# A float32 transpose of 8192 x 8192: one wait per chunk on TensorE, no branch hint, and another order of two-piece stores

## The chip, the cores and the metric

The kernel runs on one core of one Trainium2 chip. The metric is the device time of one execution in microseconds, from the first to the last work on the core; the smaller the better. Of three runs of the kernel before the median was 1263.56 us, with 1263.29 and 1263.79 at the ends.

## The reference

The input is one float32 matrix of 8192 rows and 8192 columns, 256 MiB, in HBM. The output is its transpose, of the same size. Nothing else is computed:

```python
def setup_inputs():
    return {
        "x": np.random.randn(8192, 8192).astype(np.float32),
    }

def reference(x: np.ndarray) -> np.ndarray:
    return np.transpose(x)
```

So 268 MB have to be read and 268 MB written, with a change of order between.

## The kernel before, in words

**Chunks.** The matrix is cut into two halves of 4096 columns (`s` = 0 and 1), and each half into 64 bands of 128 rows (`c`). A band of a half is a chunk: 128 rows of 16 KB each, 2 MB. There are 128 chunks, first the 64 of `s` = 0, then those of `s` = 1. The place where the second half begins, between chunk 63 and chunk 64, is the seam.

**Loads.** A chunk is loaded by one DMA into one of three input buffers `in0` to `in2`. The first three loads are issued on SyncE's queue, all later ones on ScalarE's (L102). The load of chunk t + 3 is issued once TensorE has finished chunk t and so no longer reads that buffer. The semaphore `s_ld[k]` of a buffer rises by 16 when a load has landed, one for each of the 16 DMA engines that share the transfer.

**TensorE.** It transposes a chunk in 32 pieces of 128 x 128, each a matmul with the identity (L118), into PSUM. The 32 pieces form eight blocks `q` of four. Blocks 0 to 3 go into the half of PSUM that ScalarE empties (`ps0`), blocks 4 to 7 into the half that VectorE empties (`ps1`). Ahead of a chunk stands the wait for its load (L112). Ahead of block 0 and of block 4 stands a wait for the bank (L116): the semaphores `s_banka` and `s_bankv` say that the copy engine has emptied its half of the chunk before. After every second block TensorE raises `s_pe`, on which the copies wait. TensorE's program is a loop, `turns`, of three chunks a turn and 43 turns. At the head of a turn stands a test, `now < 3`, and behind it a branch prefetch hint (L141) for the branch at the loop's end (L147). So the hint is executed in the first three turns.

**Copies.** ScalarE copies blocks 0 to 3 from PSUM into SBUF, VectorE blocks 4 to 7 (L228), each in one to four instructions as the places lie. The place is a region of `regs`, of which there are nine. A region collects one block over eight chunks, so that a row of the output gets 8 x 128 columns, 4 KB, in one piece. The eight blocks are staggered, so that one region becomes full in each chunk. The copy that is a chunk's last on its engine frees the bank.

**Stores.** When a region is full, ScalarE issues its store (L28): 512 rows of the output, 4 KB of each, 2 MB. So in the middle of the kernel ScalarE's queue carries one store and one load per chunk, in turn. In the first chunks the regions hold fewer chunks, and the stores have rows of 512 B, 1 KB and so on.

**The seam.** Seven regions are open when the first half ends. Such a region holds the last columns of 512 output rows and the first columns of 512 other rows. Its store is two DMAs: for block q the first piece has 7 − q chunks and the second q + 1, so rows of (7 − q) x 512 B and (q + 1) x 512 B. In `store` the piece of the first half is issued first. Both raise the region's semaphore, and the region is free when both have landed.

**What sets the order.** Each engine's program is written out by hand in the order shown; there is no scheduler. The transfers on ScalarE's queue start in the order of their issue. The lines that matter are `transposes` (L111 to L124), the loop (L131 to L150), `store` (L160 to L179) and the freeing of the bank (L233 to L238).

Of the kernel before, what the change touches and what calls it, by code (L numbers as in the profile page):

```python
# [40 lines left out]
def kernel(  # L41
# [13 lines left out]
    nc = tc.nc  # L55
# [9 lines left out]
    NIN = 3  # L65
# [4 lines left out]
    with tc.tile_critical():  # L70
        nc.alloc_sbuf_tensor("pad", [P, 32], dt)
        ident = nc.alloc_sbuf_tensor("ident", [P, P], dt).ap()
        ins = [nc.alloc_sbuf_tensor(f"in{k}", [P, J], dt).ap() for k in range(NIN)]
        SIZE = B * W * P
        regs = nc.alloc_sbuf_tensor("regs", [P, NREG * SIZE], dt).ap()
        NH = NR // 2
        pss = [nc.alloc_psum_tensor(f"ps{k}", [P, NH * B * P], dt).ap() for k in range(2)]

        s_id = nc.alloc_semaphore("s_id")
        s_ld = [nc.alloc_semaphore(f"s_ld{k}") for k in range(NIN)]  # L80
        s_st = [nc.alloc_semaphore(f"s_st{k}") for k in range(NREG)]
        s_bank = [nc.alloc_semaphore("s_banka"), nc.alloc_semaphore("s_bankv")]
        s_pe = nc.alloc_semaphore("s_pe")
        s_cp = [nc.alloc_semaphore("s_cpa"), nc.alloc_semaphore("s_cpv")]

        nc.gpsimd.memset(ident, 0.0).then_inc(s_id, 1)  # L86
        nc.gpsimd.wait_ge(s_id, 1)
        nc.gpsimd.affine_select(  # L88
            out=ident,
            in_=ident,  # L90
            compare_op=mybir.AluOpType.not_equal,
            fill=1.0,
            base=0,
            pattern=[[-1, P]],
            channel_multiplier=1,
        ).then_inc(s_id, 1)

        chunks = [(s, c) for s in range(M // J) for c in range(CH)]

        def load(t):  # L100
            s, c = chunks[t]
            (nc.sync if t < NIN else nc.scalar).dma_start(  # L102
                out=ins[t % NIN], in_=x[c * P:(c + 1) * P, s * J:(s + 1) * J]
            ).then_inc(s_ld[t % NIN], 16)

        def transposes(k):  # L111
            nc.tensor.sem_inc(s_ld[k], -16).wait_op(s_ld[k], 16, "sem-ge")  # L112
            for q in range(NR):
                e, g = divmod(q, NH)
                if g == 0:
                    nc.tensor.sem_inc(s_bank[e], -1).wait_op(s_bank[e], 1, "sem-ge")  # L116
                for b in range(B):
                    tr = nc.tensor.transpose(  # L118
                        pss[e][:, (g * B + b) * P:(g * B + b + 1) * P],
                        ins[k][:, q * B * P + b:(q + 1) * B * P - B + b + 1:B],  # L120
                        ident,
                    )
                if q % 2:
                    tr.then_inc(s_pe, 1)  # L124

        T = len(chunks)
        assert T % NIN == NIN - 1
        pe = [nc.tensor.engine]  # L130
        for e in range(2):  # L131
            nc.tensor.sem_inc(s_bank[e], 1)
        nc.tensor.wait_ge(s_id, 2)

        turn = nc.alloc_registers("turn", engines=pe)
        nc.regs_mov(turn, 0)
        nc.br("turns", engines=pe)
        with nc.body("turns", valid_engines=pe):
            now = nc.snap(turn, min_val=0, max_val=T // NIN)
            with nc.tensor.If(now < 3):  # L140
                hint = nc.tensor.mark_branch_hint_location()  # L141
            with nc.tensor.If(now > 0):
                transposes(NIN - 1)
            for k in range(NIN - 1):
                transposes(k)
            nc.regs_alu(turn, turn, 1, op=mybir.AluOpType.add)
            nc.tensor.br_lt(  # L147
                turn, T // NIN + 1, on_true="turns", on_false="done"
            ).branch_hint(hint)
        nc.switch_bb("done")  # L150

        for t in range(NIN):
            load(t)

        copied = [0, 0]
        free = list(range(NREG))
        stored = [0] * NREG
        window = {}

        def store(q, e, count):  # L160
            t0, r, parts = window.pop(q)
            nc.scalar.wait_ge(s_cp[e], count)
            base = 0
            for s, a, z in parts:
                rows = (z - a) * P
                j0 = s * J + q * B * P
                dst = out[j0:j0 + B * P, a * P:a * P + rows]
                dst = dst.rearrange("(q b) i -> q b i", q=P)
                src = regs[:, r * SIZE + base:r * SIZE + base + B * rows]
                base += B * rows  # L170
                if any(stored):
                    st = wide_dma(nc, nc.scalar, "qActDynamicHW", dst, src)
                else:
                    st = nc.scalar.dma_start(
                        out=dst, in_=src.rearrange("q (b i) -> q b i", b=B)
                    )
                st.then_inc(s_st[r], 16)
                stored[r] += 1
            free.append(r)  # L179

        def closes(w, t):
            t0, r, parts = w
            return t + 1 == t0 + sum(z - a for _, a, z in parts)

        for t, (s, c) in enumerate(chunks):
            for e in range(2):
                eng = (nc.scalar, nc.vector)[e]

                place = []
                for q in range(e * NH, (e + 1) * NH):  # L190
                    if q not in window:

                        span = (q - c) % W + 1
                        r = free.pop(0)
                        parts = [(s, c, min(c + span, CH))]
                        if c + span > CH and t + span < T:
                            parts.append((s + 1, 0, c + span - CH))
                        window[q] = (t, r, parts)  # L200
                        if stored[r]:
                            eng.wait_ge(s_st[r], 16 * stored[r])
                    t0, r, parts = window[q]
                    k = [p[0] for p in parts].index(s)
                    base = r * SIZE + B * P * sum(z - a for _, a, z in parts[:k])
                    _, a, z = parts[k]
                    place.append((base + (c - a) * P, (z - a) * P))

                runs = []
                for g in range(NH):  # L210
                    if runs:
                        u = runs[-1]
                        gap = place[g][0] - place[g - 1][0]
                        if place[g][1] == place[u[0]][1] and abs(gap) < 2 ** 15 and (
                            len(u) == 1 or gap == place[u[1]][0] - place[u[0]][0]
                        ):
                            u.append(g)
                            continue
                    runs.append([g])
                for u in runs:  # L220
                    off, dist = place[u[0]]
                    gap = place[u[-1]][0] - place[u[-2]][0] if len(u) > 1 else 0
                    dims = [list(regs.ap[0]), [gap, len(u)], [dist, B], [1, P]]
                    o = bass.AP(regs.tensor, regs.offset + off, dims)
                    i = pss[e][:, u[0] * B * P:(u[-1] + 1) * B * P]
                    i = i.rearrange("p (l b i) -> p l b i", b=B, i=P)
                    eng.wait_ge(s_pe, t * NH + (e * NH + u[-1]) // 2 + 1)  # L227
                    cp = nc.scalar.copy(out=o, in_=i) if e == 0 else nc.vector.tensor_copy(out=o, in_=i)  # L228
                    ends = [e * NH + g for g in u if closes(window[e * NH + g], t)]
                    if ends:  # L230
                        cp.then_inc(s_cp[e], 1)
                        copied[e] += 1
                    if u is runs[-1]:  # L233
                        if ends:
                            eng.wait_ge(s_cp[e], copied[e])
                            eng.sem_inc(s_bank[e], 1)
                        else:
                            cp.then_inc(s_bank[e], 1)  # L238
                    for q in ends:
                        store(q, e, copied[e])  # L240
            if t + NIN < T:
                nc.scalar.wait_ge(s_pe, (t + 1) * NR // 2)
                load(t + NIN)
        for r in range(NREG):
            nc.sync.wait_ge(s_st[r], 16 * stored[r])
# [30 lines left out]
```

## Time and profile before

| what | us |
|---|---|
| median of the runs | 1263.56 |
| lowest and highest | 1263.29, 1263.79 |
| span of the profiled execution | 1261.2 |
| what lies around the span, by the median | 2.4 |
| TensorE busy with matmuls, 4096 of them | 740.3 |
| VectorE busy, 250 copies | 302.7 |
| ScalarE busy, 256 copies | 251.3 |
| DMA: 537 MB in the span | 426 GB/s |

For the profiled execution the span is known; its own time with what lies around it is not listed apart from the three runs, so the 2.4 us are the median less the span.

How to read it: the span runs from the first to the last instruction. A row of the timeline or of the groups gives the line of the kernel, the engine, the operation, what is written and read, and how often. ACTq and SPq are the queues on which ScalarE and SyncE issue DMAs; PEq is TensorE's sequencer. An arrow names what ended an engine's idle time. A row of windows gives the stretch, the busy time of each engine, the granted clock of TensorE, the share of time for which the 16 DMA engines were busy, and the GB/s that they moved.

### The profile page before, as it was taken

What the parts mean: (1) busy time and instruction counts of PE and PEld (TensorE: products, weight loads), DVE (VectorE), ACT (ScalarE), POOL (GpSimd) and SP (SyncE); (2) the same over time, 40 slices, a digit from 0 to 9 for tenths busy, and PEclk for the clock granted to TensorE, in tenths of its full rate; (3) what the DMA queues carried; (4) which work ended last, traced back from release to release, by engine and by line L of the source; (5) the groups of instructions that cost most, each with busy time, mean ns of one, the idle gap of its engine ahead of it and who ended that gap; (6) DMA issues with size and microseconds to landing.
All of it is one profiled execution on the core that took longest, in us unless ns stands there. A gap on an engine that the chain in (4) does not pass through costs nothing. (4 is left out here: it accounts for less than half of the span.)

```text
span 1261.2 us, 9840 instructions
## 1 busy us (share of the span) xinstructions
PE 740.3 (59%) x4096; PEld 719.8 (57%) x4096; DVE 302.7 (24%) x250; ACT 252.6 (20%) x257; POOL 0.7 (0%) x6
## 2 busy tenths in 40 slices
PE   6555655665556565665555655656566655656561
PEld 6555555665556555655555655656566655656561
DVE  3322222222222222222222222222222222222220
ACT  3212121121111211122211121121111211122120
POOL 0000000000000000000000000000000000000000
PEclk9987867777776868687776777676867677777866
DMA  9999999999999999999999999999999999999998
GB/s 386 429 427 426 430 427 429 431 428 430 431 428 431 429 429 430 430 429 430 425 423 419 431 430 429 430 430 429 431 430 429 431 429 430 430 430 429 429 429 351
DMA packets 39273, 536.97 MB, mean 426 GB/s; under 512 B 4320, under 2 KB 4832, under 8 KB 6240
## 3 DMA queue, kind: packets, MB, share of 16 engines
q10 hardware_dynamic: 38832, 530.60, 98.9%
q1 hardware_dynamic: 432, 6.29, 1.2%
q14 instruction: 8, 0.07, 0.0%
q8 instruction: 1, 0.02, 0.0%
HBM read 268.44 MB, written 268.44 MB: 426 GB/s over the span
## 5 line engine op out<-in xcount | busy, mean ns | idle before, releaser
L118 PE MATMUL ps<-ident,in 128*128 128x128 f32 x4096 | 740.3, 363 | 492.9 <-PEq L116 492.9
L118 PEld LDWEIGHTS ps<-ident,in 128*128 128x128 f32 x4096 | 719.8, 220 | 513.2 <-issue 513.2
L228 DVE COPY regs<-ps 128x512 f32<-128x512 f32 (+3 forms) x250 | 302.7, 1246 | 932.4 <-PE ps L118 780.2
L228 ACT COPY regs<-ps 128x512 f32<-128x512 f32 (+3 forms) x256 | 251.3, 1015 | 980.9 <-PE ps L118 495.5
L228 ACT ACT_TABLE_LOAD x1 | 1.3, 1283 | 0.9 <-SPq L70 0.9
L88 POOL TENSOR_SCALAR_AFFINE_SELECT ident<-ident 128x128 f32<-128x128 f32 x1 | 0.3, 292 | 0.2 <-POOL ident L86 0.2
L86 POOL MEMSET ident<- 128x128 f32 x1 | 0.2, 204 | 0.5 <-SPq L70 0.5
L260 POOL MEMSET const-bfloat16-1.0<- 128x1 bf16 x1 | 0.1, 101 | 0.0
L260 POOL MEMSET const-uint8-127<- 128x1 uint8 x1 | 0.1, 101 | 0.0
L260 POOL MEMSET const-float32-0.0<- 128x1 f32 x1 | 0.1, 98 | 0.2 <-issue 0.2
L260 POOL MEMSET const-float32-1.0<- 128x1 f32 x1 | 0.1, 98 | 0.0
## 6 DMA issues: line engine op xcount, KB each, us to landing
in<-in_x_dram ACTq DMA_DIRECT2D x125, 2048.0 KB, 21.7
out_dram<-regs ACTq DMA_DIRECT2D x114, 2048.0 KB, 17.5
out_dram<-regs ACTq DMA_DIRECT2D x4, 1792.0 KB, 17.1
in<-in_x_dram SPq DMA_DIRECT2D x3, 2048.0 KB, 11.6
out_dram<-regs ACTq DMA_DIRECT2D x4, 1536.0 KB, 15.2
out_dram<-regs ACTq DMA_DIRECT2D x4, 1280.0 KB, 15.5
out_dram<-regs ACTq DMA_DIRECT2D x4, 1024.0 KB, 15.6
out_dram<-regs ACTq DMA_DIRECT2D x4, 768.0 KB, 16.5
```

Source lines behind the costliest of these rows:

```text
L86: nc.gpsimd.memset(ident, 0.0).then_inc(s_id, 1)
L88: nc.gpsimd.affine_select(out=ident, in_=ident, compare_op=mybir.AluOpType.not_equal, fill=1.0, base=0, pattern=[[-1, P]], channel_multipl ...
L118: tr = nc.tensor.transpose(pss[e][:, (g * B + b) * P:(g * B + b + 1) * P], ins[k][:, q * B * P + b:(q + 1) * B * P - B + b + 1:B], ident,)
L228: cp = nc.scalar.copy(out=o, in_=i) if e == 0 else nc.vector.tensor_copy(out=o, in_=i)
L260: nc = _bacc.Bacc("TRN2", target_bir_lowering=False, num_devices=1)
```

## The change

Four edits. TensorE's wait for the bank goes, and with it the semaphores `s_bank`. The copy engines now raise the load semaphore of the next chunk's buffer by one each, and TensorE waits once per chunk, for 18: the 16 of the load and one from each copy engine. For the first chunk ScalarE and VectorE raise it at the start. The test and the hint at the head of the loop go. And in `store` the pieces are collected first and issued in the order of their row lengths, the longest first; pieces of the same length keep their order. In all, 14 instructions fewer.

```diff
@@ allocation and start
-        s_bank = [nc.alloc_semaphore("s_banka"), nc.alloc_semaphore("s_bankv")]
...
+        nc.vector.sem_inc(s_ld[0], 1)
+        nc.scalar.sem_inc(s_ld[0], 1)
@@ transposes
-            nc.tensor.sem_inc(s_ld[k], -16).wait_op(s_ld[k], 16, "sem-ge")
+            nc.tensor.sem_inc(s_ld[k], -18).wait_op(s_ld[k], 18, "sem-ge")
             for q in range(NR):
                 e, g = divmod(q, NH)
-                if g == 0:
-                    nc.tensor.sem_inc(s_bank[e], -1).wait_op(s_bank[e], 1, "sem-ge")
@@ the loop
-        for e in range(2):
-            nc.tensor.sem_inc(s_bank[e], 1)
         nc.tensor.wait_ge(s_id, 2)
...
-            with nc.tensor.If(now < 3):
-                hint = nc.tensor.mark_branch_hint_location()
...
-            nc.tensor.br_lt(
-                turn, T // NIN + 1, on_true="turns", on_false="done"
-            ).branch_hint(hint)
+            nc.tensor.br_lt(turn, T // NIN + 1, on_true="turns", on_false="done")
@@ store
             base = 0
+            pieces = []
             for s, a, z in parts:
...
                 base += B * rows
+                pieces.append((rows, dst, src))
+            for rows, dst, src in sorted(pieces, key=lambda v: -v[0]):
                 if any(stored):
@@ the copies
                 eng = (nc.scalar, nc.vector)[e]
+                go = s_ld[(t + 1) % NIN]
...
                         if ends:
                             eng.wait_ge(s_cp[e], copied[e])
-                            eng.sem_inc(s_bank[e], 1)
+                            eng.sem_inc(go, 1)
                         else:
-                            cp.then_inc(s_bank[e], 1)
+                            cp.then_inc(go, 1)
```

## The prediction

> **What bounds the kernel.** I read the page's DMA queues first, then the DMA share in the windows at the start, the seam and the end, then the waits, then the timeline of the first chunks.
>
> ```profile
> span 1261.2 us, 9840 instructions
> ...
> q10 hardware_dynamic: 38832, 530.60, 98.9%
> q1 hardware_dynamic: 432, 6.29, 1.2%
> q14 instruction: 8, 0.07, 0.0%
> q8 instruction: 1, 0.02, 0.0%
> ```
>
> The two data queues together keep the 16 DMA engines busy for 98.9% + 1.2%, which is the whole span. The work is 537 MB that no edit changes. A step on TensorE, VectorE or ScalarE therefore changes the end only if a DMA engine runs out of queued packets because of it, or if it puts packets of its own on an engine.
>
> ```profile
> PE ps L118 <- PEq L116: 492.9, 127, 8.5
> ```
>
> TensorE stands still for 492.9 us in 127 waits, 3.9 us per chunk. The bank wait L116 is named because it is the last instruction before the transposes; what was really late can only be seen in the timeline. The end of the span has a slack of its own:
>
> ```profile
> 720.00:900.00 180.00, 111.34 (x596) 108.47 (x597) 41.63 (x24) 35.96 (x38) 0.00 (x0) 0.73 1.01 430
> ...
> 1254.00:1255.00 1.00, 0.00 (x0) 0.00 (x0) 0.00 (x0) 0.00 (x0) 0.00 (x0) 0.50 0.88 373
> 1255.00:1256.00 1.00, 0.00 (x0) 0.00 (x0) 0.00 (x0) 0.00 (x0) 0.00 (x0) 0.50 0.39 164
> 1256.00:1257.00 1.00, 0.00 (x0) 0.00 (x0) 0.00 (x0) 0.00 (x0) 0.00 (x0) 0.50 0.42 180
> 1257.00:1258.00 1.00, 0.00 (x0) 0.00 (x0) 0.00 (x0) 0.00 (x0) 0.00 (x0) 0.50 0.23 98
> 1258.00:1259.00 1.00, 0.00 (x0) 0.00 (x0) 0.00 (x0) 0.00 (x0) 0.00 (x0) 0.50 0.08 33
> ```
>
> The last two columns are DMA share and GB/s. In the middle all engines are busy at 430 GB/s. At the end the share falls in steps over about 4 us: the engines do not finish together, and the slowest of them ends the kernel. The four windows after 1255 hold 0.39 + 0.42 + 0.23 + 0.08 = 1.1 us of full DMA work, done in 4. If all engines finished together the end would come 4 − 1.1 = 2.9 us earlier. So what matters is time lost on the slowest engine, and the whole reserve in that is about 3 us.
>
> **The change, part by part.** First, TensorE waits once per chunk, for the load (16) and both copy engines (1 + 1). Before, its first half needed ScalarE's copies alone. New is that the first half of a chunk also waits for VectorE's copies of the chunk before. In steady state that is no wait:
>
> ```profile
> 827.79 5.56 PE L118 MATMUL ps<-ident,in 128*128 128x128 f32 x32 [4.33 <-PEq L116]
> ...
> 832.50 2.35 DVE L228 COPY regs<-ps 128x1024 f32<-128x1024 f32 x2 [7.43 <-DMA out_dram<-regs]
> ...
> 837.57 5.57 PE L118 MATMUL ps<-ident,in 128*128 128x128 f32 x32 [4.22 <-PEq L116]
> ```
>
> VectorE ends at 832.50 + 2.35 = 834.85, and TensorE starts its next chunk 2.7 us later, at 837.57. Both bank releases are there by then, so what it waits for is the load. The merged wait ends with the same event. The instructions removed (two bank waits per chunk and the hint's test) lie inside this idle time and are worth nothing; without it they would cost their own length. The two increments added at the start stand on VectorE and ScalarE ahead of their first copies, which wait for TensorE anyway: 0. The first chunks are different:
>
> ```profile
> 8.46 9.57 PE L118 MATMUL ps<-ident,in 128*128 128x128 f32 x64 [8.46 <-PEq L116]
> 13.22 2.48 DVE L228 COPY regs<-ps 128x512 f32<-128x512 f32 x4 [13.22 <-PE ps L118]
> 17.09 2.48 DVE L228 COPY regs<-ps 128x512 f32<-128x512 f32 x4 [1.39 <-PE ps L118]
> 18.06 0.33 ACTq L102 DMA_DIRECT2D in<-in_x_dram  x1
> 18.40 4.11 PE L118 MATMUL ps<-ident,in 128*128 128x128 f32 x32 [0.38 <-PEq L116]
> 21.58 2.48 DVE L228 COPY regs<-ps 128x512 f32<-128x512 f32 x4 [2.00 <-PE ps L118]
> 22.55 0.33 ACTq L102 DMA_DIRECT2D in<-in_x_dram  x1
> 24.43 5.57 PE L118 MATMUL ps<-ident,in 128*128 128x128 f32 x32 [1.93 <-PEq L116]
> 28.80 2.53 DVE L228 COPY regs<-ps 128x512 f32<-128x512 f32 x4 [4.74 <-PE ps L118]
> 30.04 0.34 ACTq L102 DMA_DIRECT2D in<-in_x_dram  x1
> 30.54 4.11 PE L118 MATMUL ps<-ident,in 128*128 128x128 f32 x32 [0.53 <-PEq L116]
> ```
>
> The first row holds chunks 0 and 1, so chunk 1 started near 8.46 + 9.57/2 = 13.2, while VectorE copied chunk 0 until 13.22 + 2.48 = 15.70. Now chunk 1 starts at 15.70, 2.5 us later. VectorE's copies of it then end at 17.09 + 2.5 + 2.48 = 22.0, and chunk 2 starts there and not at 18.40: 3.6 later. Its copies end at 21.58 + 3.6 + 2.48 = 27.7: chunk 3 is 3.3 later. Its copies end at 28.80 + 3.3 + 2.53 = 34.6: chunk 4 is 4.1 later. A chunk now takes some 6 to 7 us here, against 9.9 us that the DMA needs for one later (1261.2/128), so the delay dies out once the loads come at that pace. On ScalarE the store and the next load stand behind the copies of the late chunk and are as late. Whether that costs anything is a question of what is still queued:
>
> ```profile
> 0.00:5.00 5.00, 0.00 (x0) 0.00 (x0) 0.00 (x0) 1.28 (x1) 0.70 (x6) 1.00 0.61 213
> ...
> in<-in_x_dram ACTq DMA_DIRECT2D x1, 2048.0 KB, 10.0
> ...
> in<-in_x_dram ACTq DMA_DIRECT2D x1, 2048.0 KB, 12.2
> ...
> in<-in_x_dram ACTq DMA_DIRECT2D x1, 2048.0 KB, 14.5
> ```
>
> The last three rows are loads 3, 4 and 5, issued at 14.18, 18.06 and 22.55; the last column is the time to landing. Load 3 lands at 24.2, load 4 at 30.3, load 5 at 37.0. With the delays load 4 is issued at 18.06 + 2.5 = 20.6, 3.6 us before load 3 has landed; load 5 at 22.55 + 3.6 = 26.2, 4.1 before load 4; load 6 at 30.04 + 3.3 = 33.3, 3.7 before load 5. The first window says how long an issue needs to reach the engines: 61% of 5 us were busy, so packets began by 2 us, some 1 us after the first issue. All margins are above that, so I take 0. If the queue did run dry, each missing microsecond would cost one; the upper bound is the largest delay less its margin, 4.1 − 3.7, so 0.4 us.
>
> Second, the branch hint goes.
>
> ```profile
> L141 PEldq BRANCH_PREFETCH_HINT  x3: 31/31/50, 2.1 to 32.9; - x3
> ...
> L147 PEldq COMPARE_BRANCH  x43: 76/208/226, 16.0 to 1231.0; - x43
> ```
>
> The hint ran in 3 of 43 turns, last at 32.9 us; the branch back took at most 226 ns with it or without. The page's q8 row shows a single instruction packet of 0.02 MB in the whole run, and q14 the other eight. So 40 turns without a hint fetched at most one block. That a loop 12 instructions shorter, without any hint, still fetches one block (only earlier) or none is my reading. Estimate of its price: one engine moves 426/16 = 26.6 GB/s, so 0.02 MB hold it for 0.75 us. Bounds −0.75 (the block is not fetched, on the engine that ends last) to +0.75; I take 0.
>
> [...]
>
> Third, the seam. Seven stores there have two pieces. In the first three the longer is already first, the fourth is half and half, and in the last three (3 and 5, 2 and 6, 1 and 7 chunks) the order turns round. Bytes, descriptors and issue instructions stay.
>
> ```profile
> 612.88 1.20 ACTq L28 DMA_DIRECT2D out_dram<-regs  x2
> ...
> 655.36 1.24 ACTq L28 DMA_DIRECT2D out_dram<-regs  x2
> ...
> 676.98 2.00 ACTq L28 DMA_DIRECT2D out_dram<-regs  x2
> ...
> out_dram<-regs ACTq DMA_DIRECT2D x1, 1280.0 KB, 18.9
> ...
> 632.00:652.00 20.00, 11.26 (x66) 10.94 (x65) 4.97 (x8) 4.01 (x5) 0.00 (x0) 0.76 1.01 420
> ...
> 665.00:691.00 26.00, 12.34 (x67) 11.83 (x66) 7.21 (x9) 3.73 (x2) 0.00 (x0) 0.68 1.01 415
> ```
>
> The first pair is issued at 612.88, the fifth at 655.36 and the seventh at 676.98; the fifth's longer piece lands 18.9 us after its issue. So the pairs with the short piece first move in about 665 to 691, where the rate is 415 GB/s against 430: 26 x 15/430 = 0.91 us lost. The stretch 632 to 652, with pairs that already have the long piece first, runs at 420: over 26 us that would lose 26 x 10/430 = 0.60. Turning the order round is worth 0.3 if the three become like their mirror images and 0.9 if they cost nothing; not turning anything else, it could also cost 0.3. A mean over engines hides what the slowest loses, so I take the middle of 0.3 and 0.9, 0.6 us gained.
>
> Sum: 0 + 0 − 0.6, on a span of 1261.2, gives 1260.6. The median of the runs, 1263.56, is 2.4 above the span; so 1263.0.
>
> **Rivals.** (a) The uneven finish shrinks. For it: the reserve of 2.9 us at the end, and the seam and the fetch, which both act on single engines. Against: nothing in the rows says that the slowest engine is the one that gains. Time: 1263.56 − 0.6 − 2.9 = 1260.1 at best; it is faster by over 0.2% from a gain of 2.5 us on. (b) Slower: the branch back misses in each turn. The place is TensorE's queue q8: 42 more blocks at 0.75 us each, on one DMA engine, 31 us, so 1295. It decides from 4 misses on (4 x 0.75 = 3 us, above 0.2%). Against it are the one packet and 226 ns. (c) The new wait in the first chunks starves the DMA, or the engines drift further apart since their packets meet differently: as much as (a) the other way, 1263.56 + 2.9 = 1266.5. Against: margins of 3.6 us and more. (d) The pieces' order does nothing: 1263.6.
>
> **How the numbers follow.** From no change one can tell about 0.2%, 2.5 us. Forecast and (d) together 0.66, all within that: the bounds −0.9 − 0.75 and +0.3 + 0.75 + 0.4 put them between 1261.9 and 1265.0. (a) in full 0.20, (b) 0.05, (c) 0.09. So faster 0.20, same 0.66, slower 0.14. The range, 1260.2 to 1266.2, takes in nearly all of (a) and most of (c) and leaves (b) out.
>
> **What would show it.** In the changed profile: chunks 1 to 6 start 2 to 4 us later, each at the end of VectorE's copies, chunk 7 or 8 at its old time; the DMA share between 5 and 60 us stays near 1; q8 still has at most one packet; the stretch 665 to 691 rises from 415 towards 420 GB/s; the last windows fall off over about 4 us. I am wrong if q8 has tens of packets, if a window of the first 40 us falls below a share of 0.95 where it was not before, or if the fall at the end becomes much shorter or longer.

## The result and the profile after

The changed kernel takes 1262.47 us, median of 14 runs (1261.12 to 1263.56). The kernel before, run beside it, takes 1264.20 (1263.29 to 1264.90, 14 runs). The ratio is 0.9984, with a 95% interval of 0.9977 to 0.9991. That is 0.16% faster, 2.0 us of 1264.2 by the ratio, and between 1.1 and 2.9 us by the interval. It lies inside the 0.2% that was called no change and on the fast side of it; the forecast was a gain of 0.6 us. The forecast of the time itself, 1263.0, is only 0.5 us off, but that is partly luck: it started from 1263.56, the median of three runs, and the median of the fourteen is 0.6 us higher.

The profiled execution after took 1262.98 us, one of the slower ones of its kernel, and its span happens to be that of before, 1261.2 us. So the sum of the span cannot show the gain here; the stretches of the span can. First the windows around the seam, in the changed kernel. The last two columns are DMA share and GB/s:

```profile
612.00:632.00 20.00, 11.84 (x65) 11.52 (x64) 4.97 (x8) 4.30 (x8) 0.00 (x0) 0.67 1.00 425
632.00:652.00 20.00, 12.78 (x67) 12.45 (x67) 4.97 (x8) 4.01 (x5) 0.00 (x0) 0.67 1.02 426
652.00:665.00 13.00, 9.49 (x48) 9.33 (x47) 2.48 (x4) 2.82 (x2) 0.00 (x0) 0.63 1.01 423
665.00:691.00 26.00, 13.74 (x82) 13.25 (x81) 7.26 (x9) 4.65 (x3) 0.00 (x0) 0.83 1.01 424
691.00:720.00 29.00, 16.30 (x96) 15.82 (x95) 6.88 (x3) 5.98 (x6) 0.00 (x0) 0.79 1.01 431
```

The stretch 665 to 691, in which the pairs move whose order was turned round, runs at 424 GB/s; before it was 415. Over 26 us that is 26 x 9/430 = 0.54 us of the mean engine. The share was 1.01 in both: the engines had packets at all times, and the packets took longer before. How far a rate moves by itself can be seen in 632 to 652, where nine of the kernels of this document move the same transfers: 420 to 429 GB/s.

The first chunks, from the timeline:

```profile
8.48 6.55 PE L117 MATMUL ps<-ident,in 128*128 128x128 f32 x32 [8.48 <-PEq L113]
13.88 2.48 DVE L223 COPY regs<-ps 128x512 f32<-128x512 f32 x4 [13.88 <-PE ps L117]
15.07 0.36 ACTq L103 DMA_DIRECT2D in<-in_x_dram  x1
16.52 4.08 PE L117 MATMUL ps<-ident,in 128*128 128x128 f32 x32 [1.48 <-PEq L113]
...
20.63 0.33 ACTq L103 DMA_DIRECT2D in<-in_x_dram  x1
22.30 4.11 PE L117 MATMUL ps<-ident,in 128*128 128x128 f32 x32 [1.71 <-PEq L113]
...
26.45 0.34 ACTq L103 DMA_DIRECT2D in<-in_x_dram  x1
28.11 4.11 PE L117 MATMUL ps<-ident,in 128*128 128x128 f32 x32 [1.70 <-PEq L113]
...
54.19 5.97 PE L117 MATMUL ps<-ident,in 128*128 128x128 f32 x32 [4.44 <-PEq L113]
```

VectorE ends the copies of chunk 0 at 13.88 + 2.48 = 16.36, and TensorE starts chunk 1 at 16.52. Chunks 1 to 3 now begin at the end of VectorE's copies, each after 1.5 to 1.7 us without work, where before they began 0 to 1.9 us after the last chunk. Loads 4 and 5 go out at 20.63 and 26.45, 2.6 and 3.9 us later than before. The last row is chunk 7, at 54.19 against 52.63. The DMA share in these stretches and the total of the instruction packets:

```profile
15.00:20.00 5.00, 3.52 (x30) 3.52 (x30) 1.70 (x4) 1.60 (x4) 0.00 (x0) 1.00 1.00 400
20.00:25.00 5.00, 3.29 (x27) 3.13 (x27) 2.15 (x4) 1.95 (x5) 0.00 (x0) 1.00 1.01 366
25.00:30.00 5.00, 3.30 (x27) 3.14 (x27) 2.48 (x4) 1.34 (x3) 0.00 (x0) 1.00 0.99 424
...
q8 instruction: 1, 0.02, 0.0%
```

No stretch is short of packets, and q8 still has a single packet in 43 turns.

### The profile page after: what moved, and what is told of

The parts are those of the page before. It is cut to its first block, busy times and chain, and to the rows that moved or that the text cites. A ratio compares the mean times of both kernels' runs of the same rounds, so it can differ in the third digit from the quotient of the medians.

```text
span 1261.2 us, 9538 instructions
## 1 busy us (share of the span) xinstructions
PE 741.5 (59%) x4096; PEld 720.8 (57%) x4096; DVE 302.5 (24%) x250; ACT 252.8 (20%) x257; POOL 0.7 (0%) x6
## 3 DMA queue, kind: packets, MB, share of 16 engines
q10 hardware_dynamic: 38832, 530.60, 98.9%
```

## The experiments

Theory A says that the order of the pieces at the seam is the whole gain. Theory B gives it to the hint or to the merged wait. All ratios are to the kernel before, run beside them, with 95% intervals.

**The seam's order alone.** The kernel before, with this edit:

```diff
-                if any(stored):
+                pieces.append((rows, dst, src))
+            for rows, dst, src in sorted(pieces, key=lambda v: -v[0]):
+                if any(stored):
```

> The kernel before with one part of the change: at the seam the longer piece is stored first. Theory A (the seam's order is the whole gain): a ratio near 0.9984, as for the whole change, the stretch 665 to 691 us rises from 415 to about 424 GB/s, and the end falls off earlier. Theory B (the hint or the merged wait brings the gain, and the seam is idle): 1.0000 within 0.0007, whatever the rate of the stretch.

Measured: 0.9986 (0.9976 to 0.9997), 1263.09 against 1264.17 us. The stretch:

```profile
665.00:691.00 26.00, 15.13 (x79) 14.65 (x78) 7.26 (x9) 3.94 (x3) 0.00 (x0) 0.69 1.01 424
```

That is the gain of the whole change within the intervals, and its rate. Theory A holds so far.

**The order turned the other way.** As above, with `key=lambda v: v[0]`, so all pairs store the shorter piece first.

> The kernel before with the order turned the other way: all seven pairs store the shorter piece first, so the three pairs that had the longer first are turned round. Theory A: slower than before by about as much as the change gained, 1.0005 to 1.002, and the stretch 632 to 652 falls from 420 GB/s to 415 or below. Theory B: 1.0000 and no difference in the rates.

Measured: 1.0007 (0.9998 to 1.0016), 1265.45 against 1264.17 us. The interval just reaches 1, so the slowing is likely and not certain. The stretches leave no doubt: the mirror image of the loss has appeared in 632 to 652, at 403 GB/s and not 420, and the old one has stayed.

```profile
632.00:652.00 20.00, 10.68 (x59) 10.35 (x58) 5.06 (x8) 4.01 (x5) 0.00 (x0) 0.76 1.00 403
...
665.00:691.00 26.00, 15.16 (x83) 14.64 (x81) 7.26 (x9) 5.60 (x3) 0.00 (x0) 0.76 1.01 411
```

**The hint's removal alone.** The kernel before without these lines:

```diff
-            with nc.tensor.If(now < 3):
-                hint = nc.tensor.mark_branch_hint_location()
...
-            ).branch_hint(hint)
```

> The kernel before without the hint and its test, all else as it was. Theory A: 1.0000 within 0.0007, one instruction packet in q8 as before. Theory B (the earlier fetch of the one block is the gain): 0.998 to 0.999. If each turn fetched a block: 1.02 or more and tens of packets in q8.

Measured: 0.9999 (0.9990 to 1.0008), one packet in q8, and the seam as slow as ever:

```profile
665.00:691.00 26.00, 14.39 (x78) 13.88 (x76) 7.34 (x9) 5.17 (x3) 0.00 (x0) 0.76 1.00 410
...
q8 instruction: 1, 0.02, 0.0%
```

**The merged wait alone.** The changed kernel with hint and order put back:

```diff
+            with nc.tensor.If(now < 3):
+                hint = nc.tensor.mark_branch_hint_location()
...
-            for rows, dst, src in sorted(pieces, key=lambda v: -v[0]):
+            for rows, dst, src in pieces:
```

> The kernel before with the merged wait alone: hint and order of the stores as before. Theory A: 1.0000 within 0.0007; chunks 1 to 6 start 2 to 4 us later and the DMA share of the first 60 us stays near 1. Theory B (the merged wait is the gain, since it spreads the first chunks more evenly): 0.998 to 0.999.

Measured: 1.0002 (0.9993 to 1.0011). The chunks start late, with 1.7 us without work ahead of each, as in the changed kernel, and the stretch at the seam has 410 GB/s:

```profile
15.42 4.08 PE L117 MATMUL ps<-ident,in 128*128 128x128 f32 x32 [1.71 <-PEq L113]
...
665.00:691.00 26.00, 15.81 (x80) 15.30 (x78) 7.26 (x9) 5.59 (x3) 0.00 (x0) 0.70 1.01 410
```

So theory B falls for both edits: each alone moves nothing that can be measured, and theory A stands. Next, which pair of pieces it is.

**Only the pair of 2 and 6 chunks turned round.** In the kernel before: `for rows, dst, src in (pieces[::-1] if pieces[0][0] == 2 * P else pieces)`.

> The kernel before, with only one of the seven pairs turned round: the one of 2 and 6 chunks stores its 6 first. Theory A1 (the loss sits in the load behind a short piece followed by its long one, and for this pair almost alone): the stretch 665 to 691 us rises from 410 to 415 to about 421 to 424 GB/s, ratio 0.9985 to 0.9995. Theory A2 (each of the three pairs with the short piece first loses its share): the stretch rises by a third of the way, to 415 or so, ratio 0.9995 to 1.0000.

Measured: 0.9988 (0.9980 to 0.9997), 1262.92 against 1264.22 us.

**Only the other two turned round**, 3 and 5, and 1 and 7.

> The kernel before, with the other two pairs turned round, 3 and 5 chunks and 1 and 7; the pair of 2 and 6 stays as it was. Theory A1: the stretch 665 to 691 us stays near 411 to 415 GB/s, ratio 0.9995 to 1.0005. Theory A2: it rises two thirds of the way, to 419 or more, ratio 0.9985 to 0.9995.

Measured: 0.9998 (0.9990 to 1.0007). The stretches, first of the run with 2 and 6 turned, then of the run with the other two:

```profile
665.00:691.00 26.00, 14.67 (x78) 14.19 (x77) 7.26 (x9) 4.86 (x3) 0.00 (x0) 0.70 1.01 422
```

```profile
665.00:691.00 26.00, 12.96 (x71) 12.45 (x69) 7.22 (x9) 3.98 (x3) 0.00 (x0) 0.68 1.00 406
```

One pair of seven carries the gain; theory A2, that each pair has its share, falls. Where at that pair the time goes can be worked out from the DMA packets in the traces. The records name no engine, but nearly every packet (99.9% before and after the change) starts within 5 ns of the end of another, so the packets can be strung together into 16 chains, one per engine. A packet's extra time is then its duration over the median of its size, plus the gap ahead of it in its chain. Summed over the load that moves right behind the pair of 2 and 6 (eight packets of 16 KB per engine), it is, in us:

```
run                     order    mean of 16 engines   largest
before                  2, 6          0.41             1.30
hint gone alone         2, 6          0.51             0.77
merged wait alone       2, 6          0.60             0.87
only 3/5 and 1/7        2, 6          0.98             1.89
all short first         2, 6          0.80             1.56
  the same, mirror pair 2, 6          0.98             1.77
after                   6, 2          0.01             0.06
seam alone              6, 2          0.01             0.07
only 2/6                6, 2          0.02             0.20
```

Six of six loads behind 2 and then 6 are slow, and none of three behind 6 and then 2. The mirror pair, which stores its 6 first in ten of the runs, lost under 0.1 us in the mean in all ten and at most 0.46 on one engine. In the mirror pair the 2 belongs to the other half of the matrix, so it is the order of the sizes and not the place in the output.

**The load ahead of the pair.** The kernel before, and at the pair of 2 and 6 the load is issued ahead of both pieces:

```diff
+            if len(parts) > 1 and parts[0][2] - parts[0][1] == 2:
+                nc.scalar.wait_ge(s_pe, (t + 1) * NR // 2)
+                load(t + NIN)
```

> The kernel before, orders of the pieces as they were, but at the pair of 2 and 6 chunks the load is issued ahead of the two pieces and not behind them, so that behind the 6 come the stores of 1 and 7. Theory L (what loses time is the load that moves right behind this pair): the loss goes, the stretch 665 to 691 us rises from 410 to 415 to above 418 GB/s, ratio 0.998 to 0.9995. Theory P (the pair itself loses it, whatever comes behind): the stretch stays at 415 or below, ratio 0.9995 to 1.001.

Measured: 1.0002 (0.9992 to 1.0012), 1264.01 against 1264.07 us.

```profile
665.00:691.00 26.00, 13.50 (x82) 12.82 (x81) 6.03 (x8) 3.93 (x3) 0.00 (x0) 0.87 1.01 422
691.00:720.00 29.00, 12.92 (x80) 12.43 (x80) 7.84 (x5) 5.98 (x6) 0.00 (x0) 0.82 1.01 417
```

The stretch rises to 422, as theory L has it, but the next one falls from 430 to 417, and the time has not moved: by the packets, the next two loads behind the pairs now lose 0.30 and 0.57 us in the mean. The pair itself is not what is slow, and the loss has only gone to later loads. Neither theory holds as it was put.

**The load between the pieces.** The changed kernel, at the seam issuing the longer piece, the load, and then the shorter piece (the shorter one is put off until `load(t + NIN)` has been issued):

```diff
+            while later:
+                issue(*later.pop(0))
```

> The changed kernel, with the load of a chunk at the seam issued between the longer piece and the shorter one, for all seven pairs. If some of what the seam still loses (about 0.4 us: 424 GB/s against 430 over 26 us) comes from two stores in a row: up to 0.5 us better than the changed kernel, ratio 0.998 to 0.9985, the stretch 665 to 691 us at 426 or more. If a load between the pieces brings the loss back: 0.999 to 1.000 and the stretch at 415 or below.

Measured: 1.0011 (1.0002 to 1.0020), 1265.46 against 1264.07 us, worse than both kernels. The loss is back in other stretches:

```profile
652.00:665.00 13.00, 7.99 (x39) 7.86 (x40) 2.48 (x4) 2.28 (x2) 0.00 (x0) 0.63 1.00 401
665.00:691.00 26.00, 17.02 (x90) 16.51 (x89) 4.90 (x7) 5.60 (x3) 0.00 (x0) 0.67 1.01 423
691.00:720.00 29.00, 17.76 (x96) 17.27 (x96) 8.40 (x5) 5.98 (x6) 0.00 (x0) 0.71 1.00 405
```

Both remaining expectations for the stretch 665 to 691 missed: it was neither above 426 nor below 415, and the ratio lies above both. By the packets, the slow loads of this run stand behind 2 and then 5 chunks (0.7 us in the mean, up to 1.8) and behind 1 and then 8 (about 1.1, up to 1.5), with less behind 2 and then 7 (0.2 in the mean): putting the shorter piece off had set it in front of the next, longer store, so it is again short, long, load. It is not every such order: the stretches 632 to 652, with the load behind 1 and 6, and 665 to 691, with the one behind 4 and 5, ran at 427 and 423 GB/s. What makes a load at the seam slow stays open. Shown is that it goes with the sequence of transfers around it.

The 0.4 us that this run hoped to win need no further cause. In the traces a packet of 4 KB takes 165 ns and one of 12 KB 466, together 631, and one of 16 KB 611; the other pairs lose 19 or 20 ns in the same way. With eight packets of each piece on an engine that is 0.16 us per pair, whatever the order, or 0.4 for some two and a half pairs in 26 us.

**Whether the delay at the start is covered by the queue.** The changed kernel with loads 3 to 6 issued one chunk later:

```diff
-                nc.scalar.wait_ge(s_pe, (t + 1) * NR // 2)
+                late = t < 4
+                nc.scalar.wait_ge(s_pe, (t + 1 + late) * NR // 2)
```

> The changed kernel, with loads 3 to 6 issued one chunk later: ScalarE waits until TensorE has finished the next chunk too. If the delay of the first chunks is hidden only by what is queued (margins of 3.6 to 4.1 us by the prediction), delays of about 6 us must show: the DMA share falls below 0.9 in a window between 18 and 40 us, and the kernel is 2 to 10 us slower than the changed one, a ratio of 1.000 to 1.007. If the queue holds more than the margins say, no change from the changed kernel: 0.998 to 0.999.

Measured: 1.0079 (1.0061 to 1.0098), 1274.02 us, 11.6 over the changed kernel's 1262.47.

```profile
15.00:20.00 5.00, 4.11 (x32) 3.95 (x32) 1.67 (x4) 0.14 (x1) 0.00 (x0) 1.00 0.61 228
20.00:25.00 5.00, 2.19 (x11) 2.22 (x12) 0.98 (x2) 2.01 (x4) 0.00 (x0) 0.65 0.89 315
25.00:30.00 5.00, 4.22 (x23) 4.03 (x22) 1.78 (x3) 0.31 (x1) 0.00 (x0) 0.67 0.60 210
30.00:35.00 5.00, 2.40 (x12) 2.43 (x13) 0.70 (x2) 1.84 (x4) 0.00 (x0) 0.67 1.08 354
35.00:40.00 5.00, 4.21 (x22) 4.02 (x21) 1.99 (x4) 0.33 (x1) 0.00 (x0) 0.65 0.63 223
```

Against 430 GB/s these five windows lose 5 x (202 + 115 + 220 + 76 + 207)/430 = 9.5 us. The queue runs dry three times (shares of 0.61, 0.60 and 0.63). In these windows ScalarE, which waits for TensorE ahead of each load, works for 0.14 to 0.33 us of 5, and TensorE for 4.11 to 4.22. By the shares, the engines had no packets for 5 x (0.39 + 0.11 + 0.40 + 0.37) = 6.4 us, so the 11.6 us are more than the empty time; the rest are stretches with a share near 1 and a low rate, as from 30 to 35. So the margins were real: a delay inside them cost nothing that can be measured (the merged wait alone, 1.0002), and one beyond them cost time (11.6 us). The size was a little above the 2 to 10 us that were expected.

**The hint in every turn.** The changed kernel with `hint = nc.tensor.mark_branch_hint_location()` at the head of each turn and `.branch_hint(hint)` on the branch.

> The changed kernel with the branch hint in every turn and no test for it. If the hint only puts off the one instruction fetch: no packet in q8 before TensorE is done, and a ratio of 0.9975 to 0.999, that is the changed kernel's or up to 0.75 us better. If that fetch decides which engine ends last: clearly below the changed kernel, under 0.9975. If the hint costs time in the loop: no effect either, since TensorE stands still 3.9 us per chunk.

Measured: 0.9990 (0.9981 to 0.9999). The packets by queue:

```profile
q10 hardware_dynamic: 38832, 530.60, 98.9%
q1 hardware_dynamic: 432, 6.29, 1.2%
q14 instruction: 8, 0.07, 0.0%
HBM read 268.44 MB, written 268.44 MB: 426 GB/s over the span
```

The row of q8 is gone, but the fetch is only put off: the packet records have the same 16 KB block at 1261.26 us, just behind the end of the span of 1260.3. In the other traces it comes 1 to 3.4 us behind the first branch back without a hint, at 84.74 before the change and at 20.76 after it, and takes 0.94 to 1.0 us. The time is the changed kernel's within the intervals, so putting the fetch off is worth nothing that can be measured.

No kernel that was tried beats the changed one clearly; the seam's order alone (0.9986), 2 and 6 alone (0.9988) and the hint in every turn (0.9990) cannot be told from it.

## Why the prediction was right, and where its sizes were off

**What bounds the kernel: right.** Late chunks, a wait merged and a hint gone moved nothing that can be measured (1.0002 and 0.9999) while the queues had packets; loads so late that the queues stood empty for 6.4 us cost 11.6.

**The merged wait, 0: right.** Alone it gives 1.0002. The working was near: chunks 1, 2 and 3 were forecast for 15.7, 22.0 and 27.7 and started at 16.52, 22.30 and 28.11; loads 4 and 5 were forecast for 20.6 and 26.2 and went out at 20.63 and 26.45. One term was left out: load 3 was taken as unmoved, and it went out at 15.07 and not at 14.18, since chunk 0 took TensorE 6.55 us. It differs from run to run: with the merged wait alone chunk 0 took less, 5.30 us, and chunk 1 started at 15.42. The delay was said to be gone by chunk 7 or 8; chunk 7 was still 1.6 us late.

**The hint, 0: right,** with the reason given: one packet in the run with a hint in three turns (at 84.74 us), one packet, only earlier (at 20.76), in 43 turns without any hint, and none within the span with it in all. The block held an engine for 0.94 to 1.0 us and not for the estimated 0.75.

**The seam, −0.6: right in place and sign, too small.** The step that failed in size is the term taken from the mean over the engines, 26 x 15/430 = 0.91 us for three pairs, of which a part would stay. The part that went was 0.54 us in the mean (415 to 424 GB/s), inside the bounds of 0.3 and 0.9; the 0.4 that stayed are, by the estimate above, the smaller packets, whose times (165 ns for 4 KB, 466 for 12) are the same before and after. But the kernel got 1.1 to 2.9 us faster, and 0.4 to 3.0 with the order alone. The prediction had the sentence, that a mean hides what the slowest loses, and then took a value from the mean all the same. In the load behind the pair the engine that lost most lost 1.30 us in the profile before, and 0.77 to 1.89 in the others, one and a half to three times the mean. That this is what the time gained besides is likely and not shown: in three of the slow traces (before, only 3/5 and 1/7, all short first) the most was lost by an engine that ran behind the others, in the other two (hint gone, merged wait) the engines behind lost 0.3 to 0.7, near the mean. The low end of the interval for the order alone would also fit the mean. It was also wrong about which pairs: it spread the loss over three, and one carries it.

**Rival (a), the uneven finish shrinks: not shown.** The windows after 1255 us in the changed kernel, to be read against those of before:

```profile
1255.00:1256.00 1.00, 0.00 (x0) 0.00 (x0) 0.00 (x0) 0.00 (x0) 0.00 (x0) 0.50 0.46 197
1256.00:1257.00 1.00, 0.00 (x0) 0.00 (x0) 0.00 (x0) 0.00 (x0) 0.00 (x0) 0.50 0.31 131
1257.00:1258.00 1.00, 0.00 (x0) 0.00 (x0) 0.00 (x0) 0.00 (x0) 0.00 (x0) 0.50 0.19 82
1258.00:1259.00 1.00, 0.00 (x0) 0.00 (x0) 0.00 (x0) 0.00 (x0) 0.00 (x0) 0.50 0.08 33
```

They hold 1.0 us in 4, as before 1.1, and the fall is no shorter. In the kernel with the seam's order alone it is:

```profile
1255.00:1256.00 1.00, 0.00 (x0) 0.00 (x0) 0.00 (x0) 0.00 (x0) 0.00 (x0) 0.50 0.50 213
1256.00:1257.00 1.00, 0.00 (x0) 0.00 (x0) 0.00 (x0) 0.00 (x0) 0.00 (x0) 0.50 0.39 164
1257.00:1258.00 1.00, 0.00 (x0) 0.00 (x0) 0.00 (x0) 0.00 (x0) 0.00 (x0) 0.50 0.12 49
1258.00:1259.00 1.00, 0.00 (x0) 0.00 (x0) 0.00 (x0) 0.00 (x0) 0.00 (x0) 0.50 0.00 0
```

Here it takes 3 us and not 4, and the span of that execution is 1260.1 us. Each is one execution; the spans of the changed kernel's runs go from 1259.3 to 1261.8, and whether the quick ones finish more evenly was not profiled. **Rivals (b) and (c)** did not come. The fetch in each turn, of which (b) made 31 us, no run shows: 43 turns without a hint had one packet in q8. Nor was a queue empty: the share from 15 to 30 us was 0.99 to 1.01. **Rival (d)**, that the order does nothing, is excluded by the interval of the order alone (0.9976 to 0.9997).

## What to carry to other kernels

Where the DMA queues are full for the whole span, as here with 98.9% and 1.2%, ask of a change only two things: does it put or slow packets on some DMA engine, and does it delay an issue past the landing of what is queued ahead. Compute the second from issue and landing times, as a margin; in this kernel a delay below it cost nothing that can be measured (1.0002), and one beyond it cost 11.6 us, more than the 6.4 that the queues stood empty. And read a loss engine by engine: 0.4 to 1.0 us in the mean were 0.8 to 1.9 on the engine that lost most.

## What was not expected of the hardware

The order of two stores of the same bytes changed the time of the load behind them: with rows of 1 KB and then of 3 KB the next 2 MB load took 0.4 to 1.0 us longer in the mean of the engines and up to 1.9 us on one, six times in six; with 3 KB and then 1 KB, under 0.1 in the mean and at most 0.5 on one. Behind the neighbours the load lost less in that place: in the trace before, about 0.15 us in the mean behind 1.5 KB and 2.5 KB and 0.01 behind 512 B and 3.5 KB. Moving the load or the short piece elsewhere moved the loss to other loads (417, 401 and 405 GB/s in stretches that had 423 to 431). Why, no run here shows.
